# One step of a two-layer hybrid decoder on one core: v projected ahead of the row lists, the sample search, packing and list steps set further apart, and the sample queries copied right behind their rotation

## The chip, the cores and the metric

The kernel runs on one core of a Trainium2 chip. The metric is device time in microseconds (us) of one execution. TensorE is written PE, its weight loads PEld, VectorE DVE, ScalarE ACT, GpSimd POOL, and SyncE SP (which only issues transfers here).

## The reference, cut to what matters

A prompt of 256 tokens and 8 sequences with 4 new tokens each (288 columns in all) go through one attention layer, one convolution layer and two feed-forward blocks. The change lies in the attention layer, which chooses its keys:

```python
q, k, v, qi, ki, wi = project_attn(x, w_in)          # five projections of the same 288 tokens
q, k, qi, ki = rope_all(q, k, qi, ki, pos)           # partial rotation
ki_past = cache_ki[page_table].reshape(Bd, PAST_LEN, IDX_DIM)      # 2048 old index keys a sequence
...
dots = jnp.einsum('thd,sd->ths', qi, ki)             # index scores: 16 heads of 64
score = jnp.einsum('th,ths->ts', wi * IDX_W_SCALE, jax.nn.relu(dots))
_, idx = lax.top_k(jnp.where(causal, score, -jnp.inf), k_sel)      # 64 keys (prompt), 256 keys (samples)
...
k_s = jnp.where(in_past, cache_k[phys, off], k_new[new_idx])       # chosen rows of the paged cache
v_s = jnp.where(in_past, cache_v[phys, off], v_new[new_idx])
return attend_selected(q_s, k_s, v_s, valid)
```

For the 32 sample tokens the choice becomes a list of 256 cache rows each, and these rows (keys and values together, 1 MB a token) are gathered from memory.

## The kernel before, in words

**Matmuls.** Each weight matrix is split into a high and a low part, and three matmuls (L230, L231, L232) of 128x128 by 288 columns make one product. `pump` keeps weights ahead: SP loads a slab of 512 KB into `raw` (L147, five buffers), ACT makes the high part `wh` (L161), and DVE, or POOL where the slab's `pool` flag is set, makes the low part `wl` (L163; three buffers of each, made two slabs ahead). A slab of a 512-column group holds two k-tiles of four outputs, a slab of a v group four k-tiles of two: 24 matmuls either way. The v weights have 2 groups of 8 slabs, each q group has 8 slabs.

**Order by hand.** Every engine takes its instructions in program order. The program is one long sequence of groups: index key, k, two groups of index queries `qi`, four groups of q, and then v. Beside them run "lanes", lists of Python generators. After every small batch of matmuls `tick` gives each lane a credit, 0.3675 for a k-tile of one output (capped at 3.0 when it is saved up), and a generator goes on when its lane's credit is above zero; the number it yields is what its next step has to wait for. So a yield of 1.5 sets the next step four or five batches of three matmuls further on in the program. A q group hands out 64 batches, 23.52 credits. A v group would hand out three ticks for every four k-tiles of one output: 24 ticks, 8.82 credits. What is left in a lane at the end is emitted at once by `drain`, with no matmuls between its steps.

**The lanes at the change.** `rope_qi` rotates the index queries of one group on DVE, first the 32 sample columns, then the 256 prompt columns. `load_kx` asks SP for the 8 gathered parts of the index-key cache at fixed credits (`KXD`). `prompt_index` scores the prompt (two halves) and picks 64 keys in 16 rounds of `max` and `match_replace` (L1026, L1027), `TOPK` credits apart. `sample_index` copies the rotated sample queries into a block layout (L814, L817), makes 16 index dot products on PE (L839, each with an ACT relu and a weighted sum L830), then finds the 256th value of each row by 32 counting steps (DVE counts at L886, PE sums the counts over the partitions at L868, `BIS` credits apart), ranks ties, packs the chosen codes to the left in 9 steps (L943 to L946), shifts the four lists of a row together in 8 steps (L970, L971), turns them by PE (L977) into `idxS`, and calls `kv_load`, which has POOL issue two gathers (L657) for every token as far as buffers allow.

**After the drain** the stage's memory and PSUM banks are given back. `kv_load` goes on to 7 tiles, the two v groups run (L230 to L232 into `sc` and `m`, ACT copies to `vT`, PE transposes L1103, DVE copies L1105), then two more tiles reuse the memory of the low part of x (`kvx`, allowed only when v has been projected), and POOL clears `qz` and `PTz` (L1119). The prompt's attention is a generator too (`filler`): `HEAD` credits of it stand ahead of the sample loop, the rest inside it. The loop takes the 32 sample tokens in turn: four PE transposes twice a token (L1188), scores (L1209), and for every four tokens softmax and values (L1252). A tile's buffer is free when its values are done, and then the gather nine tokens further on is issued.

Of the kernel before, what the change touches and what calls it, by code (L numbers as in the profile page):

```python
# [7 lines left out]
F32 = mybir.dt.float32  # L8
# [4 lines left out]
AF = mybir.ActivationFunctionType  # L13
# [5 lines left out]
TP = 256  # L19
NS, TS = 8, 4  # L20
T = TP + NS * TS
# [16 lines left out]
NKVB = 3  # L38
# [3 lines left out]
SDEL = 6  # L42
TOPK = 1.0
DGP = 6.0
NDG = 10
CQ = 287
KXD = (54.0, 5.2)
PRW = (6.0, 14.0, 9.0)
DOT = 1.0
HEAD = 8.0  # L50
PEM, NACT = 3, 4
BIS = (1.3, 0.2)
ROPE = 0.5
# [482 lines left out]
def trunk(ctx, tc, a, o, stages=9):  # L536
    k = K(ctx, tc, a, o)
    nc = k.nc
# [7 lines left out]
    g_q = [k.add(Group([(win, QC + 512 * i, 512)], [128] * 4, NT, 2)) for i in range(4)]  # L546
    g_v = [k.add(Group([(win, VC + 256 * i, 256)], [128] * 2, NT, 4)) for i in range(2)]
    for g in g_q[1:3]:
        for s_ in g.slabs:
            s_.pool = True  # L550
# [56 lines left out]
    pb = pg  # L607
# [3 lines left out]
    bp = stB.enter_context(tc.tile_pool(name="idx", bufs=1))  # L611
# [29 lines left out]
    ident = k.ident = base.tile([128, 128], F32, name="ident")  # L641
# [40 lines left out]
    kxl, pl_ = Lane(), Lane()  # L682
# [3 lines left out]
    xin = lambda kk: (xh[:, kk, :T], xl[:, kk, :T])  # L686
# [5 lines left out]
    turned = []  # L692
# [10 lines left out]
    def rope_qi(gi):  # L703

        for c0, n in ((TP, T - TP), (0, TP)):
            wide = lambda v: cc(v)[:, None, c0:c0 + n].to_broadcast([128, 4, n])
            yield from rope(qi[:, 4 * gi:4 * gi + 4, c0:c0 + n], R[:, :, c0:c0 + n], wide("ci"), wide("si"), SHUF_I,
                            lambda: turned.append(gi))

# [27 lines left out]
    ps = k.gemm(g_idx[0], xin, pg)  # L737
# [8 lines left out]

    kvt = {"pos": 0, "done": 0, "cap": 4}
    RING = 4 + NKVB + 2
# [57 lines left out]

    def sample_index():
        while 1 not in turned:
            yield 0.3
        for s in range(2):  # L810
            for par in range(2):
                src = qi[par * 64:(par + 1) * 64, :, TP:].rearrange("p j (r s t) -> p r s j t", s=2, t=TS)[:, :, s]
                dst = qb[s * 64:(s + 1) * 64].rearrange("p r (s j e t) -> p r s j e t", s=2, e=2, t=TS)[:, :, s, :, par]
                nc.vector.tensor_copy(dst, src)  # L814
        kn = bp.tile([128, 4, TS], F32, name="kn")
        for s in range(2):
            nc.vector.tensor_copy(kn[s * 64:(s + 1) * 64],  # L817
                                  ki[s * 64:(s + 1) * 64, TP:].rearrange("p (r s t) -> p r s t", s=2, t=TS)[:, :, s])
        p = pb()
        nc.tensor.matmul(p[:, :32], cc("esel", 64, 80), kiw[64:80, TP:], start=True, stop=True)  # L820
# [62 lines left out]
        for bit in range(30, -1, -1):  # L883
# [32 lines left out]
        nc.vector.tensor_tensor_scan(rank, eq, eq, 0.0, OP.add, OP.max)  # L916
        yield 1.5

# [6 lines left out]
                                cc("blk", 96, 128).rearrange("p (b t) -> p b t", t=TS), op=OP.max)  # L925
        yield 1.5

# [12 lines left out]
        for b in range(9):  # L940
            s_ = 1 << b
            m = sp.tile([128, 512], I32, name="m_", tag="w", bufs=3)
            nc.vector.tensor_scalar(m, x_, 1 << (15 + b), None, op0=OP.bitwise_and)  # L943
            y = sp.tile([128, 512], I32, name="x_", tag="w", bufs=3)
            nc.vector.scalar_tensor_tensor(y, m, 0.0, x_, op0=OP.is_equal, op1=OP.mult)
            nc.vector.copy_predicated(y[:, :512 - s_], m[:, s_:], x_[:, s_:])  # L946
            x_ = y
            yield 2.4

# [17 lines left out]
        for b in range(8):  # L967
            s_ = 1 << b
            y = sp.tile([128, KSEL_S], F32, name="lst", tag="w", bufs=3)
            nc.vector.tensor_scalar(y, lst, b0[:, b:b + 1], None, op0=OP.mult)  # L970
            nc.vector.scalar_tensor_tensor(y[:, s_:], lst[:, :KSEL_S - s_], b1[:, b:b + 1], y[:, s_:],  # L971
                                           op0=OP.mult, op1=OP.add)
            lst = y
            yield 1.3
        p = pb()
# [91 lines left out]
    def post_q(h):  # L1067
        return lambda: nc.gpsimd.tensor_copy(qn[:, h], q[:, 4 * h:4 * h + 4, TP:].rearrange("p g t -> p t g"))

    for gi in range(4):  # L1070
        ps = k.gemm(g_q[gi], xin, pg)
        evac_rope(2 * gi + 2, ps, [q[:, 4 * gi + m] for m in range(4)], post_q(gi))
    k.drain(k.ev, k.bg2, k.bg, kxl, pl_)
    k.lanes.remove(kxl)
# [12 lines left out]
    def bank(n, bufs):  # L1087
        return pp.tile([128, 512], F32, name=n, bufs=bufs)

    kvt["B"], kvt["cap"] = kvB, 4 + NKVB  # L1090
    kv_load(0)
    for gi in range(2):
        n_ = ("sc", "m")[gi]
        ps = k.gemm(g_v[gi], xin, lambda: bank(n_, 2))
        vT = cp.tile([128, 2, T], F32, name="vT", tag="PT", bufs=2)
        for m in range(2):
            nc.scalar.activation(vT[:, m], ps[m][:, :T], AF.Copy)
        nc.sync.dma_start(o["v"].rearrange("(j p) t -> p j t", p=128)[:, 2 * gi:2 * gi + 2], vT)
        for tt in range(3):
            n = 128 if tt < 2 else 32  # L1100
            p = bank("tr", 3)
            for m in range(2):
                nc.tensor.transpose(p[:n, m * 128:m * 128 + 128], vT[:, m, tt * 128:tt * 128 + n], ident)  # L1103
            dst = vt[:, tt] if tt < 2 else vs
            nc.vector.tensor_copy(dst[:, 256 * gi:256 * gi + 256], p[:n, :256])  # L1105

# [759 lines left out]
```

## Time and profile before

| what | value |
|---|---|
| three timed runs | 2685.71, 2688.73, 2689.75 us; median 2688.73 |
| profiled execution | 2684.9 us; span from first to last instruction 2683.1 us |
| PE busy | 2568.1 us, 96% of the span |
| DVE, ACT, POOL busy | 1624.3, 1160.8, 615.2 us |
| mean granted TensorE clock | 0.984 of full speed |

The page cuts the span into 40 slices of 67 us. In PE's line of tenths the first seven slices read 8899688, all later ones but one 9; the granted clock falls below 9 tenths in the sixth slice alone. The attention layer is the first 470 us of the span, and all that the change touches is in it.

### The profile page before, as it was taken

To read this page: it belongs to the slowest core of one execution; us is meant where nothing else is said; L and a number is where in the kernel's file an instruction comes from. 1 tells how busy PE (TensorE), PEld (TensorE's weight loads), DVE (VectorE), ACT (ScalarE), POOL (GpSimd) and SP (SyncE) were. 2 spreads that over 40 slices of the span, in tenths; PEclk is the share of its full clock that TensorE was granted. 3 is DMA by queue.
4 is the path that set the end of the run, shared out by engine and by line. 5 is a ranking of instruction groups with operands and counts; after the bars stand their busy time and mean duration, and the time that the engine had idled before them with its cause. 6 is when DMAs were issued, how large, how long until landed. Compare 5 with 4: busy or idle time off the path is not lost.

```text
span 2683.1 us, 49547 instructions
## 1 busy us (share of the span) xinstructions
PE 2568.1 (96%) x19608; PEld 2464.8 (92%) x19608; DVE 1624.3 (61%) x2546; ACT 1160.8 (43%) x1801; POOL 615.2 (23%) x857
## 2 busy tenths in 40 slices
PE   8899688999999999999999999899999999999997
PEld 8779555999999999999998889899999999999997
DVE  4568443668666445555557888778655544555554
ACT  4333233456444334444446444656444333444434
POOL 1023324243222110111126444443111000111123
PEclk9999799999999999999999999999999999999999
DMA  9834636556554555555554766555555445555653
GB/s 342 181 87 131 227 131 244 185 168 197 162 172 156 167 166 165 159 172 164 158 165 128 201 161 175 171 157 161 171 165 165 165 160 164 172 165 159 167 169 106
DMA packets 410552, 454.90 MB, mean 170 GB/s; under 512 B 34816, under 2 KB 338608, under 8 KB 409168
## 3 DMA queue, kind: packets, MB, share of 16 engines
q1 hardware_dynamic: 397920, 400.66, 49.3%
q0 software_dynamic: 12400, 51.09, 5.7%
q8 instruction: 153, 2.51, 0.4%
q14 instruction: 79, 0.65, 0.1%
HBM read 438.37 MB, written 13.30 MB: 168 GB/s over the span
## 4 chain that ended last, share of the span: by engine, by line
PE 85%; DVE 4%; issue 3%; DMA 2%; POOL 2%; ACT 2%; SPq 1%; another core or an unknown queue 0%; ACTq 0%; DVEq 0%; POOLq 0%
PE pt L231 25%; PE pt L232 25%; PE pt L230 25%; PE pg L230 2%; PE pg L232 2%; PE pg L231 2%; DVE wl L163 1%; PE pt L1652 1%; ACT wh L161 1%; POOL kvt L657 1%; PE tr L1188 1%; DMA kvt<-kvc,idxS 1%; PE pg L839 1%; DMA xt<-spread 1%; PE m L1252 0%
## 5 line engine op out<-in xcount | busy, mean ns | idle before, releaser
L163 DVE TENSOR_TENSOR wl<-raw,wh 128x1024 fp32r<-128x1024 f32 (+2 forms) x709 | 883.9, 1250 | 816.5 <-ACT wh L161 796.2
L161 ACT ACTIVATE wh<-raw 128x1024 fp32r<-128x1024 f32 (+1 forms) x726 | 760.4, 1051 | 939.8 <-PE pt L231 684.0
L232 PE MATMUL pt<-xh,wl 128*128 128x288 f32 (+1 forms) x3520 | 1040.7, 296 | 5.4 <-DVE wl L163 5.4
L230 PE MATMUL pt<-xh,wh 128*128 128x288 f32 (+1 forms) x3520 | 1043.2, 296 | 0.8 <-ACT xh L1311 0.8
L231 PE MATMUL pt<-xl,wh 128*128 128x288 f32 (+1 forms) x3520 | 1043.1, 296 | 0.1
L232 PEld LDWEIGHTS pt<-xh,wl 128*128 128x128 f32 x3520 | 666.9, 189 | 6.6 <-DVE wl L163 6.6
L230 PEld LDWEIGHTS pt<-xh,wh 128*128 128x128 f32 x3520 | 664.0, 189 | 7.4 <-issue 5.4
L231 PEld LDWEIGHTS pt<-xl,wh 128*128 128x128 f32 x3520 | 664.7, 189 | 0.5 <-DVE xl L1312 0.3
L232 PE MATMUL pt<-hh,wl 128*128 128x288 f32 (+1 forms) x1664 | 495.3, 298 | 2.9 <-DVE wl L163 2.9
L231 PE MATMUL pt<-hl,wh 128*128 128x288 f32 (+1 forms) x1664 | 495.0, 297 | 0.0
L230 PE MATMUL pt<-hh,wh 128*128 128x288 f32 (+1 forms) x1664 | 493.2, 296 | 1.2 <-ACT wh L161 1.2
L232 PEld LDWEIGHTS pt<-hh,wl 128*128 128x128 f32 x1664 | 312.8, 188 | 3.9 <-DVE wl L163 3.9
L230 PEld LDWEIGHTS pt<-hh,wh 128*128 128x128 f32 x1664 | 313.8, 189 | 2.4 <-ACT wh L161 2.1
L231 PEld LDWEIGHTS pt<-hl,wh 128*128 128x128 f32 x1664 | 313.6, 188 | 0.2
L1427 POOL COPY sto<-gpad 128x2 f32<-128x2 f32 x88 | 82.0, 932 | 963.6 <-ACT gpad L1420 963.5
L230 PE MATMUL pg<-xh,wh 128*128 128x288 f32 (+1 forms) x464 | 148.4, 320 | 8.2 <-ACT wh L161 7.7
L232 PE MATMUL pg<-xh,wl 128*128 128x288 f32 (+1 forms) x464 | 139.6, 301 | 1.8 <-DVE wl L163 1.7
L231 PE MATMUL pg<-xl,wh 128*128 128x288 f32 (+1 forms) x464 | 139.8, 301 | 0.1
L1431 ACT ACTIVATE s<-y,pvec 128x304 f32<-128x304 f32 x88 | 48.4, 550 | 162.0 <-DVE y L1426 162.0
L230 PEld LDWEIGHTS pg<-xh,wh 128*128 128x128 f32 (+1 forms) x464 | 88.8, 191 | 18.0 <-issue 8.7
L305 POOL TENSOR_TENSOR lns<-lns,x 128x288 f32<-128x288 f32 x56 | 53.0, 947 | 184.4 <-DVE x L1340 176.9
L232 PEld LDWEIGHTS pg<-xh,wl 128*128 128x128 f32 (+1 forms) x464 | 89.0, 192 | 3.1 <-DVE wl L163 3.1
(389 smaller groups left out, 2428.2 us busy)
## 6 DMA issues: line engine op xcount, KB each, us to landing
raw<-w_ffn_gate SPq DMA_DIRECT2D x352, 256.0 KB, 2.9
raw<-w_ffn_up SPq DMA_DIRECT2D x352, 256.0 KB, 3.2
raw<-w_ffn_down SPq DMA_DIRECT2D x169, 512.0 KB, 3.9
raw<-w_attn_in SPq DMA_DIRECT2D x64, 512.0 KB, 5.4
raw<-w_pw SPq DMA_DIRECT2D x128, 256.0 KB, 4.4
raw<-w_attn_out SPq DMA_DIRECT2D x32, 512.0 KB, 4.3
raw<-w_pw SPq DMA_DIRECT2D x32, 512.0 KB, 4.2
xt<-spread SPq DMA_DIRECT2D x60, 136.0 KB, 3.1
```

What stands on the lines that cost most here:

```text
L161: nc.scalar.activation(wh[:, :n], r[:, :n], AF.Copy)
L163: eng.tensor_tensor(wl[:, :n], r[:, :n], wh[:, :n].bitcast(F32), op=OP.subtract)
L230: nc.tensor.matmul(out, wh[:, c:c + w], xh, start=st, stop=False)
L231: nc.tensor.matmul(out, wh[:, c:c + w], xl, start=False, stop=False)
L232: nc.tensor.matmul(out, wl[:, c:c + w], xh, start=False, stop=sp)
L305: nc.gpsimd.tensor_tensor(self.s1, self.s1, self.x[:, j], op=OP.add)
L657: nc.gpsimd.indirect_dma_start(out=out, out_offset=None, in_=src, in_offset=bass.IndirectOffsetOnAxis(ap=idx, axis=0))
L839: nc.tensor.matmul(p[:, :512], qb[:, pr], kx[pr][:, 512 * i:512 * i + 512], start=True, stop=True)
L1188: nc.tensor.transpose(p[:, h * 128:(h + 1) * 128], g[:, h * 128:(h + 1) * 128], ident)
L1427: nc.gpsimd.tensor_copy(sto[:, j, 0:2], gp[:, 256:258])
L1431: nc.scalar.activation(s[:, :304], y[:, :304], AF.Silu, bias=k.par(bc, j))
L1652: nc.tensor.matmul(p[32 * i:32 * i + 32, :TP], dg[:, i, m - PEM], xt[:, i, 4 * (m - PEM):4 * (m - PEM) + TP], start=m == PEM, stop=m == 7, ...
```

## The change

1. The v groups move from behind the drain to behind the four q groups, ahead of it. Their output goes to the memory of `qi`, and the transposes become a generator `turn_v` in a lane, with copies on ACT in place of DVE. The lists are drained after the second v group.
2. Distances in program order: search steps 1.3 + 0.2 to 1.6 + 0.3, ranking 1.5 to 2.5 and 1.5 to 2.0, packing 2.4 to 2.9, list steps 1.3 to 1.4, top-k rounds 1.0 to 1.6, and the index dot products 1.0 to 0.35, with a wait of 5.0 ahead of the first.
3. The sample queries' copies (L814, L817) are issued by `rope_qi` right after the sample columns of the second group, ahead of the prompt columns.
4. The eight loads of index keys are asked for from 53.0 on, 4.8 apart (before: 54.0 and 5.2).
5. The low parts of the first four slabs of the fourth q group are made on POOL. The copies `qn` of the sample queries (L1068) move from POOL to ACT.
6. `HEAD` goes from 8 to 10, and `kv_load` issues two tiles before the memory is given back, not four.

```diff
-TOPK = 1.0
+TOPK = 1.6
-KXD = (54.0, 5.2)
+KXD = (53.0, 4.8)
-DOT = 1.0
-HEAD = 8.0
+DOT = 0.35
+HEAD = 10.0
+DOTW = 5.0
-BIS = (1.3, 0.2)
+BIS = (1.6, 0.3)
...
-    for g in g_q[1:3]:
-        for s_ in g.slabs:
+    for g in g_q[1:]:
+        for s_ in g.slabs[:8 if g is not g_q[3] else 4]:
             s_.pool = True
...
-                            lambda: turned.append(gi))
+                            lambda: turned.append(gi) if c0 else None)
+            if c0 and gi:
+                sample_queries()
...
-    kvt = {"pos": 0, "done": 0, "cap": 4}
+    kvt = {"pos": 0, "done": 0, "cap": 2}
...
+    def sample_queries():
         for s in range(2):
             for par in range(2):
...
+    def sample_index():
+        while 1 not in turned:
+            yield 0.3
+        yield DOTW
...
         nc.vector.tensor_tensor_scan(rank, eq, eq, 0.0, OP.add, OP.max)
-        yield 1.5
+        yield 2.5
...
                                 cc("blk", 96, 128).rearrange("p (b t) -> p b t", t=TS), op=OP.max)
-        yield 1.5
+        yield 2.0
...
             x_ = y
-            yield 2.4
+            yield 2.9
...
             lst = y
-            yield 1.3
+            yield 1.4
...
-        return lambda: nc.gpsimd.tensor_copy(qn[:, h], q[:, 4 * h:4 * h + 4, TP:].rearrange("p g t -> p t g"))
+        return lambda: nc.scalar.activation(qn[:, h], q[:, 4 * h:4 * h + 4, TP:].rearrange("p g t -> p t g"), AF.Copy)
...
-    k.drain(k.ev, k.bg2, k.bg, kxl, pl_)
+    vT = bp.tile([128, 8, T], F32, name="qi")
+    def turn_v(gi):
+        for tt in range(3):
+            n = 128 if tt < 2 else 32
+            p = pb()
+            for m in range(2):
+                nc.tensor.transpose(p[:n, m * 128:m * 128 + 128], vT[:, 2 * gi + m, tt * 128:tt * 128 + n], ident)
+            dst = vt[:, tt] if tt < 2 else vs
+            nc.scalar.activation(dst[:, 256 * gi:256 * gi + 256], p[:n, :256], AF.Copy)
+            yield 0.6
+    for gi in range(2):
+        ps = k.gemm(g_v[gi], xin, pg)
+        for m in range(2):
+            nc.scalar.activation(vT[:, 2 * gi + m], ps[m][:, :T], AF.Copy)
+        nc.sync.dma_start(o["v"].rearrange("(j p) t -> p j t", p=128)[:, 2 * gi:2 * gi + 2], vT[:, 2 * gi:2 * gi + 2])
+        if gi:
+            k.drain(k.ev, k.bg2, kxl, pl_, k.bg)
+        pl_.append(turn_v(gi))
+    k.drain(pl_)
```

The v groups' old place, with their copies of `vT` on DVE, is taken out.

## Rows read from the trace of the kernel before

**Rows 1.** What PE waited for, first 400 us: us in total, times, longest

```profile
PE pg L977 <- DVE lst L970: 11.7, 1, 11.7
PE pg L839 <- issue: 8.9, 1, 8.9
...
PE pg L868 <- DVE scr L886: 5.3, 4, 3.5
PE pg L868 <- ACT x L726: 4.0, 1, 4.0
```

**Rows 2.** Stretches of 10 us: each engine's busy time, granted clock, DMA share, GB/s

```profile
110.00:120.00 10.00, 5.17 (x11) 3.13 (x12) 5.12 (x11) 1.19 (x2) 0.00 (x0) 0.54 0.28 69
...
220.00:230.00 10.00, 10.00 (x79) 10.00 (x78) 7.11 (x33) 3.18 (x3) 6.24 (x4) 1.00 0.50 139
...
240.00:250.00 10.00, 6.02 (x37) 5.81 (x37) 8.78 (x18) 5.11 (x11) 0.92 (x1) 0.87 0.31 97
...
260.00:270.00 10.00, 10.00 (x77) 10.00 (x77) 9.69 (x15) 3.73 (x5) 0.00 (x0) 1.00 0.48 134
...
300.00:310.00 10.00, 4.12 (x18) 3.53 (x18) 3.53 (x5) 2.60 (x4) 2.48 (x3) 0.60 0.94 343
```

**Rows 3.** DVE in order of time, 107 to 115 us: start, duration, instruction

```profile
107.75 0.29 DVE L695 STREAM_SHUFFLE rsh<-qi 128x128 f32<-128x128 f32 x1
...
112.53 1.22 DVE L699 TENSOR_TENSOR qi<-qi,rsh 128x1024 f32<-128x1024 f32 x1
113.68 0.92 DVE L814 COPY qiblk<-qi 64x128 f32<-64x128 f32 x4
```

**Rows 4.** DMA issues between 60 and 130 us, median to landing

```profile
kvt<-kid SPq DMA_DIRECT2D x8, 512.0 KB, 11.0
```

**Rows 5.** DVE by line and shape, 60 to 284 us: count, busy us, mean ns

```profile
L163 DVE TENSOR_TENSOR wl<-raw,wh 128x1024 fp32r<-128x1024 f32 x28 | 34.0, 1224 | 45.4 <-ACT wh L161 45.2
...
L1026 DVE MAX8 m<-pacc 128x8 f32<-128x256 f32 x8 | 3.4, 422 | 0.1
L1027 DVE MATCH_REPLACE8 pacc<-m,pacc 128x256 f32<-128x256 f32 x8 | 3.3, 410 | 0.0
```

**Rows 6.** DVE in order of time: a rotation, the list steps, the finished list

```profile
174.32 0.46 DVE L720 TENSOR_TENSOR rsh<-rsh,con 128x288 f32<-128x288 f32 x1
174.69 2.60 DVE L721 TENSOR_TENSOR rsh<-rsh,con 128x288 f32<-128x288 f32 x1
...
279.09 0.35 DVE L970 TENSOR_SCALAR lst<-lst,b 128x256 f32<-128x256 f32 x1
...
279.99 0.35 DVE L970 TENSOR_SCALAR lst<-lst,b 128x256 f32<-128x256 f32 x1
...
284.11 0.22 DVE L980 TENSOR_SCALAR idxS<-pg 128x64 int32<-128x64 f32 x1 [0.77 <-PE pg L977]
```

**Rows 7.** POOL in order of time: a low part, first and fourteenth gather, clearing

```profile
174.43 2.55 POOL L163 TENSOR_TENSOR wl<-raw,wh 128x1024 fp32r<-128x1024 f32 x1 [3.37 <-ACT wh L161]
...
284.62 1.79 POOL L657 DMA_INDIRECT kvt<-kvc,idxS  x1 [7.66 <-DVE idxS L980]
...
302.16 0.93 POOL L657 DMA_INDIRECT kvt<-kvc,idxS  x1 [0.31 <-issue]
...
327.58 0.58 POOL L1119 MEMSET qz<- 128x256 f32 x2
```

**Rows 8.** PE in order of time, from the first v matmul into the loop

```profile
284.48 0.58 PE L230 MATMUL sc<-xh,wh 128*128 128x288 f32 x1 [0.41 <-DVE idxS L980]
...
306.51 1.63 PE L1103 MATMUL tr<-ident,vT 128*128 128x128 f32 x6 [5.12 <-ACT vT L1097]
...
324.13 0.22 PE L1137 MATMUL tr<-pm,identN 128*128 128x128 bf16 x1
...
344.03 0.60 PE L1188 MATMUL tr<-ident,kvt 128*128 128x128 f32 x4
...
373.94 0.63 PE L1188 MATMUL tr<-ident,kvt 128*128 128x128 f32 x4 [0.47 <-DMA kvt<-kvc,idxS]
```

More of the change, by code (lines that the diff above doesn't have):

```diff
@@ L805, in prepare @@
         yield 0.1
-    def sample_index():
-        while 1 not in turned:
-            yield 0.3
+    kn = bp.tile([128, 4, TS], F32, name="kn")
+    def sample_queries():
         for s in range(2):
@@ L814, in sample_index @@
                 nc.vector.tensor_copy(dst, src)
-        kn = bp.tile([128, 4, TS], F32, name="kn")
         for s in range(2):
@@ L1088, in bank @@
         return pp.tile([128, 512], F32, name=n, bufs=bufs)
-    kvt["B"], kvt["cap"] = kvB, 4 + NKVB
+    kvt["B"] = kvB
+    kvt["cap"] = 4 + NKVB
     kv_load(0)
[L1092 to L1105, printed above, removed]
     ot = q
```

## The prediction

> **What bounds the kernel now.** I read the page first: PE is busy in nearly every slice except in the first 470 us, so I asked for stretches of 10 us there and then for what PE waited on. Four holes stand out. (1) PE does nothing for 8.9 us in front of the first index dot product, L839 [rows 1]; the releaser is not named, but DVE's order of time shows it: the rotation of the sample columns begins at 107.75, yet the copies that L839 needs come at 113.68 and end at 114.6, behind four long instructions on the prompt columns, of which the last stands in the rows [rows 3]. So the hole is from 105.9 to 114.8. The clock is granted at 0.54 in that stretch [rows 2]. (2) The counting search waits 5.3 us for its DVE counts [rows 1], at about 170 to 180 us, where search steps, top-k rounds and a rotation meet. (3) At 243 to 247 PE waits 4.0 us [rows 1]; the row names ACT, but the sum behind it needs the count of the packing scan, which DVE reaches late, as a rotation stands ahead of it; the clock is 0.87 there [rows 2]. (4) After the last q matmul PE waits 11.7 us for the list steps [rows 1]; the list is read out at 284.11 [rows 6], about 1 us behind the end of that wait, so q ends at about 271.3. Then come v and the gathers together: first v matmul at 284.48, first attention matmul at 324.13, 39.65 us for what is 192 matmuls and 12 transposes [rows 8]; in the stretch at 300 PE is busy 4.12 us of 10 while the DMA engines are at 0.94 [rows 2]: v's weights come in behind the gathers. The head of prompt attention takes from 324.13 to 344.03, and the tokens begin [rows 8].
>
> **The change part by part.** I count credits from the first q matmul: q ends at 4 x 23.52 = 94.1, v would end at 94.1 + 2 x 8.82 = 111.7. Where matmuls run free PE does 77 in 10 us [rows 2], so a slab of 24 takes 3.12 us, a credit of a q group 1.06 us and one of a v group 1.41 us.
>
> *Copies behind the sample rotation, dots later.* The lane has 3.0 saved, so the 5.0 leaves 2.0 credits, then 1.5: the first dot stands 3.7 credits or 3.9 us of matmuls behind 105.5, at 109.4. The sample rotation is four instructions of about 0.29 us from 107.75 on, it ends at about 108.9, and the copies take 0.92 more [rows 3]: ready at about 109.9. Of 8.9 us some 0.5 is left: 8.4 gained. The prompt's rotation moves back by the copies' 1.3 us; the next low part behind it is due only after two slabs and a dozen dots. The clock: a mean of 0.54 over 10 us, between levels of 1.0 and 0.5, is 9.2 us at the low level (1.2 GHz), so PE worked from 114.8 to 120 at half speed and lost 2.6 us; with no hole before it I give that back. Sum 11.0. Bounds: 8.4, if the clock falls all the same, and 12.
>
> *Index-key loads.* Load 8 moves from credit 14.0 to 10.2. What is moved past is SP's queue: a key load lands 11.0 us after issue [rows 4], and a raw slab of the same size behind it waits. Matmuls of slabs already landed hide it: 0, at worst one load of 512 KB ahead of one slab, at the 343 GB/s of the stretch at 300 [rows 2] 1.5 us.
>
> *Search and top-k.* With low parts on POOL the search alone keeps DVE busy 7.11 us of 10 [rows 2], at 1.5 credits a step; at 1.9 that is 5.6. A late top-k round is 422 + 410 ns [rows 5], 0.78 of DVE's time at 1.0 credit, 0.49 at 1.6. Together 1.49 becomes 1.05: still over one, and over a longer overlap. The search starts at credit 12.8 (dots end at 11.6, as load 8 is at 10.2), before at 19.2; top-k runs to 36.5, before 26.9. The excess before, 7.7 credits at about 1.2 us by 0.49, is 4.5 us plus q's rotation with its 2.60 us instruction. After: 12 credits by 0.05, under 1 us, two low parts of 1.22 us each [rows 5] near the start, and the same rotation, some 5 us, against slack of about 1.9 us in a step: 3 us left of 5.3. I take a gain of 2; bounds -5 (all of the surplus of a longer overlap on PE) and +5.3.
>
> *Four slabs to POOL.* Each takes 1.22 us from DVE [rows 5] and 2.4 to 2.6 us of POOL [rows 7], which has 3.1 a slab. The row says something else too: while POOL had its low part from 174.43 on, DVE's L721 took 2.60 us, where its like just before took 0.46 [rows 6, 7]: 2.15 us lost. The Trainium skill, "SBUF — State Buffer", section "Who interferes with whom", has it that a DVE instruction with two SBUF inputs and a GpSimd one that reads SBUF block each other, the later one fully; the trace agrees in this pair. By that rule four more slabs could cost four such blocks, 8.6 us of DVE, where the saving is 4.9; by the rows it happened to one of the rotation's instructions with 16 such slabs around, so I keep the gain above and count this in its lower bound.
>
> *Ranking later.* The packing scan comes at credit 79.7 (12.8 + 60.8 + 1.6 + 2.5 + 2.0), 9 behind the start of q's last group, out of the rotation's way, where before it fell at 71.5, one credit behind it. The 4.0 us go, and about 0.5 of clock: 4.5. Bounds 0 and 5.3.
>
> *Packing, lists, and v.* First packing step at 81.2, then 9 x 2.9 and 1.2: lists begin at 108.5, and at 111.7 three of eight are out. Five are left at 0.90 us [rows 6], with one under way 5.4 in place of 11.7: 6.3 gained. Before, packing and low parts filled DVE to 9.69 of 10 [rows 2]; 2.9 instead of 2.4 makes room for the low parts that remain, and in v a slab gives only 2.2 credits in 3.12 us. Bounds 0 (nothing shortened) and 9.
> v itself: 192 / 7.7 = 24.9 us, transposes at 1.63 for six at the low clock [rows 8], together 2.5: 27.4 for 39.65, 12.2 gained, rounded to 12. The weights no longer meet the gathers, since these are issued after. Bounds 6 (if the 5.9 us hole of the stretch at 300 comes back) and 13. The copies of v and q on ACT (3.18 us of 10 busy at 220 [rows 2]) cost nothing; if ACT were late, low parts would be late next.
>
> *Bare gathers.* Now nothing but the head covers them. The list should be ready at about 286 (284.1 - 11 - 2 - 4.5 - 6.3 + 24.9 + 0.8), 2 us later than before, and the head starts 2 us behind that, not 40. POOL needs 17.54 / 13 = 1.35 us a gather [rows 7], 18 of them and the clearing of `qz`: done at 286 + 24.9 + 0.6 = 311.5. The head takes 19.9 us [rows 8], plus the two further yields of `HEAD` = 10: about 24, ending at 312. So the tokens begin at about 311, the two conditions level. The two yields stood inside the first token before: 0, bounds -4 and 0. The first nine tokens took 344.03 to 373.94 [rows 8]; nine tiles and 3.7 MB of the next weights at 343 GB/s [rows 2] are 13.1 MB in 38 us, so tile 8 lands by about 327 and is wanted at 336: 0. From tile 9 on a gather waits for its buffer in both kernels.
>
> Sum: 11 + 2 + 4.5 + 6.3 + 12 = 35.8. From the profiled 2684.9 that is 2649.1; the median of the runs is 3.8 higher, 2652.9 by the same gain. I take 2651.
>
> **The rivals.**
> *DVE stays the bound*: search and top-k overlap longer, POOL blocks DVE more often, and holes 2 and 3 are as deep as before or deeper. For: 1.05 is over one [rows 2, 5]. Against: in q's second and third group DVE had a third of its time free. With -5 and 0 for those terms the sum is 24.3: 2662. Chance 0.17.
> *The list's tail stays*: DVE comes to the end of v late, 11.7 us again: 2657. For: 9.69 of 10 busy. Chance 0.10.
> *The first hole stays*, moved: the dots wait for the key loads or for the weights behind them. For: 11.0 us to landing [rows 4]. Sum 24.8: 2662. Chance 0.06.
> *Tiles late*: with 200 GB/s in place of 343, 13.1 MB take 65 us, tile 8 lands at 351 and not 336, 15 us: 2666. Against: the rate of the same gathers [rows 2]. Chance 0.08.
> *Slower*: the gathers are held up one by one by DVE, as L721 was by POOL, now that the head's softmax runs beside all 18. At 2.15 us more each [rows 6] `qz` is cleared at 286 + 18 x 3.5 + 0.6 = 350, six behind the 344 of before, and the tokens' own gathers suffer too: about 2695. It decides from 32.5 / 18 = 1.8 us more a gather. The Trainium skill, on the same page under "SBUF: two separate sides", warns of this: descriptors of GpSimd's transfers cannot be written while DVE holds the shared ports. Against it: the gathers came at an even 1.35 us [rows 7] with DVE at work on low parts, though not on softmax. Chance 0.04.
> *Nothing comes of it*, as tokens wait for tiles by all that was won: 0.02.
>
> **How the numbers follow.** My forecast has 0.53: 2651, its own range 2643 to 2658. The rivals at 2657 to 2666 are taken in, and a little on the lower side for bounds not reached (12, 5.3, 5.3, 9 and 13 give 44.6, 2640): 2640 to 2667 leaves out under 2 in 10. About 0.2%, 5 us, is what a measurement of this kernel can tell. Faster 0.93, the same 0.03, slower 0.04.
>
> **What the changed profile would show.** No wait of L839 over 1 us near 106 and a granted clock of 1.0 to 130; waits of L868 summing to 3 or 4 us; the wait of L977 at 5 to 6 us, around 280; v's matmuls in 25 us with no stretch under 9 of 10; gathers from about 286 in an even row; first L1188 near 311, and everything behind the attention loop some 36 us earlier. The prediction is wrong if DVE reads 9 of 10 and more from 115 to 150 with PE below, if L977 waits 10 us, if POOL's gathers spread beyond 1.5 us, or if L1188 waits for DMA in its first nine tokens.

## The result, and the profile after

The changed kernel takes 2661.59 us (median; 2660.16 to 2664.78), the kernel before, beside it, 2688.94 us: ratio 0.9902, 95% interval 0.9885 to 0.9919, or 27.3 us. I had said 2651, a gain of 35.8. The profiled execution takes 2662.52 us (before 2684.9), its span is 2660.7, its mean clock 0.986.

After the change the lines are numbered up to 16 higher: low parts L164, index dots L846, counts L893 with their sums L875, list steps L977, list matmul L984, `idxS` L987, gathers L658; in the head the scores are L1154, row maxima L1155, transposes L1180, values L1176; key transposes are L1204. What PE waits for, first 400 us, against [rows 1]:

```profile
PE q L1176 <- ACT PT L1182: 17.7, 4, 12.3
...
PE pg L984 <- DVE lst L977: 5.1, 1, 5.1
PE pg L875 <- DVE scr L893: 3.9, 5, 0.9
...
PE pg L875 <- DVE cnt L938: 1.5, 1, 1.5
```

The wait of the index dots (8.9 us) is gone, the list wait is 5.1 where it was 11.7, and the counting sums wait 3.9 + 1.5 and another 0.8 in a shorter row, 6.2 in all for 10.3 (5.3 + 4.0 and another 1.0). Above all of them stands a wait that the kernel before did not have in this size: 12.3 us in the head of the prompt's attention. Stretches of 10 us, against [rows 2]:

```profile
110.00:120.00 10.00, 9.99 (x43) 5.53 (x44) 6.41 (x9) 4.31 (x7) 0.00 (x0) 1.00 0.76 164
...
240.00:250.00 10.00, 10.00 (x78) 10.00 (x77) 9.77 (x14) 3.47 (x4) 0.00 (x0) 1.00 0.46 130
260.00:270.00 10.00, 10.00 (x76) 9.72 (x76) 9.04 (x14) 5.50 (x9) 0.00 (x0) 1.00 0.37 102
300.00:310.00 10.00, 1.16 (x6) 0.76 (x5) 0.00 (x0) 0.00 (x0) 7.13 (x10) 0.67 1.03 420
```

The clock is whole where it had been 0.54 and 0.87. The first gap closes with the copies of the sample queries, which DVE now makes at 108.87 and not at 113.68 [rows 3]:

```profile
108.87 0.93 DVE L817 COPY qiblk<-qi 64x128 f32<-64x128 f32 x4
```

From 300 to 310 PE is busy 1.16 us, and DVE and ACT not at all, while the DMA engines move 420 GB/s. PE in order of time (start, duration, instruction; in brackets the idle time before it and its releaser), against [rows 8]:

```profile
283.32 1.06 PE L984 MATMUL pg<-con,lst 128*128 128x32 f32 x4 [5.14 <-DVE lst L977]
...
286.18 0.27 PE L1153 MATMUL tr<-pm,identN 128*128 128x128 bf16 x1 [0.46 <-ACT vt L1091]
...
299.56 0.74 PE L1154 MATMUL tr<-kT,x 128*128 128x128 f32 x2
300.10 1.06 PE L1180 MATMUL tr<-ident,P 128*128 128x128 f32 x4
313.47 2.08 PE L1176 MATMUL q<-PT,vt 128*128 128x512 f32 x2 [12.31 <-ACT PT L1182]
...
324.86 0.67 PE L1204 MATMUL tr<-ident,kvt 128*128 128x128 f32 x4
```

The list is turned at 283.32, the head begins 2.9 us later, and the first key transpose comes 38.7 us after that, where I had 24. DVE in the hole, in order of time:

```profile
295.38 0.95 DVE L1165 TENSOR_SCALAR P<-P,sm 128x128 f32<-128x128 f32 x4
310.41 0.69 DVE L1155 TENSOR_REDUCE mx<-tr 128x4 f32<-128x512 f32 x1 [14.08 <-remote]
```

L1155 reads what the L1154 matmuls wrote, and these had ended at 300.3. It starts 10 us later, and its row names no engine of the core as releaser ("remote": the profile knows none). The trace also records when an engine's reports arrive, the semaphore updates by which it tells the others that an instruction is done. PE's five reports of the matmuls L1154 and L1180, which end from 300.31 to 301.16, are recorded from 310.39 to 310.52, all at once. So DVE did not wait for work that was late, but for word of work that was done.

POOL and the tiles were as forecast; its order of time, against [rows 7]:

```profile
284.93 1.06 POOL L658 DMA_INDIRECT kvt<-kvc,idxS  x1 [53.89 <-DVE idxS L987]
...
306.27 0.94 POOL L658 DMA_INDIRECT kvx<-kvc,idxS  x1 [0.31 <-issue]
307.20 0.58 POOL L1135 MEMSET qz<- 128x256 f32 x2
```

18 gathers in 21.3 us, 1.25 from one to the next.

### The profile page after: what moved, and what is told of

Read it like the earlier page. It is cut to its first block, busy times and chain, and to the rows that moved or that the text cites. A ratio compares the mean times of both kernels' runs of the same rounds, so it can differ in the third digit from the quotient of the medians.

```text
span 2660.7 us, 49550 instructions
## 1 busy us (share of the span) xinstructions
PE 2561.8 (96%) x19608; PEld 2459.0 (92%) x19608; DVE 1617.9 (61%) x2536; ACT 1164.6 (44%) x1811; POOL 623.8 (23%) x857
## 4 chain that ended last, share of the span: by engine, by line
PE 87%; DVE 5%; DMA 2%; POOL 2%; ACT 2%; issue 1%; another core or an unknown queue 1%; SPq 0%; DVEq 0%; ACTq 0%; POOLq 0%
PE pt L233 25%; PE pt L232 25%; PE pt L231 25%; PE pg L231 2%; PE pg L233 2%; PE pg L232 2%; DVE wl L164 1%; PE tr L1204 1%; PE pt L1668 1%; ACT wh L162 1%; PE m L1268 1%; PE sc L1225 1%; DMA xt<-spread 1%; PE pg L846 1%
## 5 line engine op out<-in xcount | busy, mean ns | idle before, releaser
L164 DVE TENSOR_TENSOR wl<-raw,wh 128x1024 fp32r<-128x1024 f32 (+2 forms) x705 | 880.3, 1252 | 778.9 <-ACT wh L162 763.7
L231 PE MATMUL pg<-xh,wh 128*128 128x288 f32 (+1 forms) x528 | 166.4, 315 | 8.1 <-ACT wh L162 8.1
L233 PE MATMUL pg<-xh,wl 128*128 128x288 f32 (+1 forms) x528 | 157.6, 298 | 1.5 <-DVE wl L164 1.4
L232 PE MATMUL pg<-xl,wh 128*128 128x288 f32 (+1 forms) x528 | 157.4, 298 | 0.0
L231 PEld LDWEIGHTS pg<-xh,wh 128*128 128x128 f32 (+1 forms) x528 | 99.8, 189 | 17.3 <-issue 8.4
L233 PEld LDWEIGHTS pg<-xh,wl 128*128 128x128 f32 (+1 forms) x528 | 99.9, 189 | 2.8 <-DVE wl L164 2.8
L232 PEld LDWEIGHTS pg<-xl,wh 128*128 128x128 f32 (+1 forms) x528 | 99.9, 189 | 2.4 <-issue 2.4
```

What stands on the lines that cost most here:

```text
L164: eng.tensor_tensor(wl[:, :n], r[:, :n], wh[:, :n].bitcast(F32), op=OP.subtract)
L231: nc.tensor.matmul(out, wh[:, c:c + w], xh, start=st, stop=False)
L232: nc.tensor.matmul(out, wh[:, c:c + w], xl, start=False, stop=False)
L233: nc.tensor.matmul(out, wl[:, c:c + w], xh, start=False, stop=sp)
```

## The experiments

The result above is group 1, the first pair of runs. Twelve kernels then ran in three more groups, each on one chip beside runs of the kernel before. That kernel took 2688.94 us in the first group, 2669.3 in the second, 2684.35 in the third and 2670.94 in the fourth, so times are compared inside a group, and across groups by ratios alone. The changed kernel itself was not run in the second group, and the kernel before was traced in the first and third alone. Where the groups differ is one of the findings. A table of places, read from PE's order of time in each trace (us from the start of the span; "next layer" is the first matmul of the output projection):

| kernel | group | first index dot | list turned | head begins | first key transpose | next layer |
|---|---|---|---|---|---|---|
| before | 1 | 114.83 | 283.01 | 324.13 | 344.03 | 468.37 |
| changed | 1 | 110.01 | 283.32 | 286.18 | 324.86 | 448.03 |
| changed, HEAD 8 | 2 | 110.92 | 284.14 | 286.99 | 308.54 | 428.24 |
| changed, gathers paced | 2 | 110.70 | 283.98 | 286.84 | 314.75 | 430.53 |
| before, early copies alone | 2 | 109.72 | 270.06 | 303.63 | 324.77 | 439.17 |
| changed, v at its old place | 2 | 110.54 | 271.78 | 304.86 | 332.67 | 450.43 |
| before | 3 | 115.60 | 284.66 | 324.25 | 343.16 | 468.67 |
| changed | 3 | 110.67 | 285.40 | 288.26 | 324.86 | 447.11 |
| changed, HEAD 8 | 3 | 110.28 | 283.53 | 286.38 | 318.86 | 449.67 |
| changed, late copies | 3 | 114.61 | 291.47 | 294.33 | 332.11 | 455.23 |
| changed | 4 | 110.77 | 284.02 | 286.88 | 315.01 | 429.56 |
| changed, gathers paced | 4 | 111.09 | 284.36 | 287.21 | 315.17 | 431.38 |
| changed, paced, HEAD 8 | 4 | 110.97 | 285.69 | 288.55 | 311.52 | 427.68 |
| changed, old distances | 4 | 110.29 | 276.65 | 299.89 | 327.83 | 442.67 |

**Group 2: the head, and two halves of the change.** The head with its old share:

```diff
-HEAD = 10.0
+HEAD = 8.0
```

> The changed kernel with HEAD back at 8.0. Theory A, the two further yields of the head cost what the trace shows ahead of the first token and are hardly given back inside the loop: the first key transposes come 5 to 6 us earlier, the loop is 1 us longer, total 4 to 5 us less than the changed kernel, about 2657. Rival, as the prediction had it, the two yields only change place: the loop is longer by as much as the head is shorter, total unchanged within 1 us. The hole of 12 us in the head stays in both.

Measured: 2640.31 us, ratio 0.9895 (0.9878 to 0.9911). The head takes 21.6 us, and the wait of 12 us, which I had expected to stay, is not there: the longest in front of the values is 2.6.

The gathers spread out, two tiles ahead of the head and two more after each softmax (the copy of `sm` makes POOL wait for it):

```diff
-    kvt["cap"] = 4 + NKVB
-    kv_load(0)
...
-    kvt["B2"], kvt["cap"] = base.tile([128, 2, 2, 1024], F32, name="kvx", tag="xl"), RING
-    kv_load(0)
+    kvt["B2"] = base.tile([128, 2, 2, 1024], F32, name="kvx", tag="xl")
+    pace = cp.tile([128, 4], F32, name="pace", bufs=1)
...
+            if kvt["cap"] < RING:
+                nc.gpsimd.tensor_copy(pace, sm)
+                kvt["cap"] = min(RING, kvt["cap"] + 2)
+                kv_load(0)
```

> The changed kernel with the first nine tiles' gathers paced: two tiles at once, then two more after each of the first four softmax units of the head (POOL copies a result of DVE first, so it really waits), and qz and PTz cleared ahead of them. Theory A, the 12 us hole in the head comes from 18 gathers standing in the DMA queues at once, and updates of TensorE reach DVE late while they drain: the wait of L1176 for L1182 falls from 17.7 us to under 8, the head from 38.7 to about 28, total about 2651. Rival B, the hole is a wait of its own at the third unit of the head (memory or a bank given over): it stays at 12 us, total unchanged, 2661. Rival C, paced gathers come too late: the hole goes, but L1204 waits for DMA in the first nine tokens by as much.

Measured: 2643.95 us, ratio 0.9906 (0.9889 to 0.9923), head 27.9. By itself this says nothing on the cause: HEAD 8 had lost the hole in this group too, with all 18 gathers in one burst.

The kernel before, with early copies, closer dots and earlier key loads alone:

```diff
-KXD = (54.0, 5.2)
+KXD = (53.0, 4.8)
-DOT = 1.0
+DOT = 0.35
+DOTW = 5.0
...
+            if c0 and gi:
+                sample_queries()
```

> The kernel before with only the early copies, the dots' distances and the key loads of the change. Theory: the hole of 8.9 us at 106 goes and the clock stays up, 11 us; the search begins some 6 credits earlier and so the list's tail is shorter by about 5 us as well: 2672 to 2675. Rival, the first hole is only moved (the dots wait for key loads, or the low parts behind the rotation are late): under 5 us gained, 2684 or more.

Measured: 2658.74 us, ratio 0.9962 (0.9950 to 0.9975): 10.6 us, where my term was 11.0. PE's waits in that kernel:

```profile
PE pg L984 <- DVE lst L977: 9.8, 1, 9.8
...
PE pg L875 <- DVE scr L893: 4.1, 5, 1.3
```

The list comes 12.9 us earlier than in the kernel before of group 1 (no trace of that kernel in this group): 11.0, and 1.9 because the list wait shrinks from 11.7 to 9.8.

The changed kernel with v back behind the drain:

```diff
-    vT = bp.tile([128, 8, T], F32, name="qi")
-    def turn_v(gi):
...
-    for gi in range(2):
-        ps = k.gemm(g_v[gi], xin, pg)
...
+    k.drain(k.ev, k.bg2, k.bg, kxl, pl_)
...
+    for gi in range(2):
+        n_ = ("sc", "m")[gi]
+        ps = k.gemm(g_v[gi], xin, lambda: bank(n_, 2))
```

> The changed kernel with v projected behind the drain again, beside the gathers, all else kept. Theory: with the wider spacing five packing steps and eight list steps are left at the end of q, a tail of about 17 us instead of 5; v takes 40 us beside the gathers instead of 28, but the 12 us hole in the head is then inside v's stretch: net 12 to 16 us slower than the changed kernel, 2674 to 2678. Rival, moving v is worth only the tail's cover and the hole appears in the head as well: 24 us slower, 2686.

Measured: 2661.44 us, ratio 0.9972 (0.9962 to 0.9981), which cannot be told from the early copies alone: what is set further apart has to be paid in the tail. By ratios it is 18 us above the changed kernel, where I expected 12 to 16 (the tail about 17 us, as it came, and 40 us for v, where it took less). Its list wait, and three of its stretches behind it:

```profile
PE pg L984 <- DVE lst L977: 18.0, 1, 18.0
```

```profile
280.00:290.00 10.00, 9.61 (x74) 9.32 (x73) 4.21 (x6) 3.89 (x5) 7.87 (x8) 1.00 0.98 379
290.00:300.00 10.00, 10.00 (x77) 10.00 (x76) 2.91 (x4) 2.12 (x2) 2.67 (x3) 1.00 0.99 360
300.00:310.00 10.00, 6.10 (x47) 5.23 (x45) 5.85 (x7) 2.26 (x6) 6.00 (x8) 1.00 0.88 299
```

Here v's matmuls run beside the gathers at 360 to 379 GB/s, as in [rows 2], and PE has no hole. From the list's matmul to the head it takes 33.1 us (33.6 with the early copies alone), in the kernel before 41.1. So v's weights behind the gathers were not what held PE in the kernel before.

**Group 3: the hole again.** The kernel before once more, unchanged:

> The kernel before, unchanged, for a trace on the chip that the other runs of this call use. Theory A (while a burst of gathers drains, other engines' reports come late, and whether they do depends on the chip): if this chip is like that of the second group of runs, no row of 290 to 310 us names an unknown releaser with 10 us, first v matmul to first attention matmul takes 32 to 33 us in place of 39.65, and the execution takes about 2669 us; if it is like the chip of the first pair, the row is there again and it takes about 2686. Theory B (the stretch at 300 us belongs to the program: v's weights behind the gathers): 39 to 40 us on either chip.

Measured: 2682.82 us in the one run; 39.6 us from list to head. ACT in order of time, first the kernel before from which the prediction was made, then this run:

```profile
293.76 1.06 ACT L161 ACTIVATE wh<-raw 128x1024 fp32r<-128x1024 f32 x1 [3.18 <-PE sc L232]
305.11 1.06 ACT L161 ACTIVATE wh<-raw 128x1024 fp32r<-128x1024 f32 x1 [10.29 <-remote]
```

```profile
306.05 1.06 ACT L161 ACTIVATE wh<-raw 128x1024 fp32r<-128x1024 f32 x1 [9.59 <-remote]
```

Ten microseconds without a named releaser in the middle of v: the same kind of row as in the head of the changed kernel. In the first of the two traces, PE's matmuls ahead of it had ended at 295.88 and 296.01, and their reports are recorded at 305.08 and 305.12. The weights had long been there. v has eight slabs (two groups of four; 192 matmuls), and the DMA issues of the kernel before from 250 to 272 us, ahead of the first gather at 284.62, hold seven of them, with 3.7 us to landing:

```profile
raw<-w_attn_in SPq DMA_DIRECT2D x7, 512.0 KB, 3.7
```

The slab of the late row had landed by 272.22.

The changed kernel once more:

> The changed kernel, unchanged. Theory A on a chip without late reports: the hole of 12.3 us in front of the value matmuls shrinks to about 7, as in the runs with HEAD 8 and with paced gathers; head 28 us in place of 38.7 (HEAD 8 took 21.6, two more yields some 6); time about 2646, ratio to before 0.991. On a chip with late reports as in the first pair: head 38 to 39 us, ratio 0.990. Theory B (the hole is an own wait of the head's third unit, of the program's order): 12 us again on either chip, ratio about 0.995 beside a before of 2669.

Measured: 2659.28 us, ratio 0.9904 (0.9887 to 0.9921). The wait in front of the values is 10.9 us, and DVE's L1155 again starts behind 12.69 us put down to "remote".

HEAD 8 once more (the same edit, beside the changed kernel of this group):

> The changed kernel with HEAD 8 in place of 10, beside the changed kernel on the same chip. Theory that the two further yields stand on the path, since the tiles wait in their buffers by then: 5 to 6 us quicker than the changed kernel, some 1 given back in the loop: 4 to 5 us. Rival (what my prediction said: the yields stood inside the first tokens before, and cost nothing): within 1 us.

Measured: 2660.47 us, ratio 0.9903 (0.9885 to 0.9921): no difference, where I expected 4 to 5 us. The head has the hole too (L1155 behind 13.99 us put down to "remote") and takes 32.5 us for 36.6. The first key transpose comes 6 us earlier than with HEAD 10, 1.9 of it from the stretch ahead of the head, but the next layer 2.6 us later. Its stretches in the tokens, and a row of ACT there:

```profile
360.00:370.00 10.00, 6.76 (x83) 3.99 (x81) 3.26 (x11) 2.21 (x7) 6.39 (x7) 1.00 0.91 307
370.00:380.00 10.00, 9.06 (x75) 5.88 (x76) 3.09 (x9) 3.10 (x6) 0.95 (x2) 0.66 0.30 114
```

```profile
370.29 0.60 ACT L1209 ACTIVATE KT<-tr 128x512 f32<-128x512 f32 x1 [1.55 <-remote]
```

A row of that kind stands in the next burst of gathers; PE loses 3.2 us from 360 to 370, and then the clock falls to 0.66.

The sample queries' copies back behind the rotation of the prompt columns:

```diff
-            if c0 and gi:
-                sample_queries()
...
         yield DOTW
+        sample_queries()
```

> The changed kernel with the sample queries' copies issued behind the rotation of the prompt columns again (and behind the wait of 0.3 steps), everything else as changed. Theory that the copies' place made the first hole: a wait of PE of 3.5 us or more in front of the first index dot product (copies ready at about 114, dots placed at 109.5), clock low behind it, first dot near 114.5, time 7 to 11 us above the changed kernel. Rival (the wider distances and the lane's saved credit alone closed it, or a later wait takes up the delay, as v's end and the list are slack): below 3 us.

Measured: 2669.48 us, ratio 0.9943 (0.9926 to 0.9959), 10.2 us above the changed kernel. PE's wait, and DVE in order of time:

```profile
PE pg L845 <- issue: 4.7, 1, 4.7
```

```profile
108.57 1.34 DVE L696 STREAM_SHUFFLE rsh<-qi 128x1024 f32<-128x1024 f32 x1
...
113.48 0.92 DVE L815 COPY qiblk<-qi 64x128 f32<-64x128 f32 x4
```

The first dot comes at 114.61, 3.9 us late, and the clock of the stretch from 110 to 120 reads 0.66. So the copies' place made the first hole; distances do not close it.

**Group 4: without the hole.** The changed kernel a third time:

> The changed kernel, unchanged, beside the three that follow on one chip. If the chip has late reports: ratio 0.990, a wait of 10 to 12 us in front of the value matmuls of the head. If it has none: ratio about 0.991 and 7 us there.

Measured: 2644.15 us, ratio 0.9904 (0.9886 to 0.9922), head 28.1. DVE's same instruction, and the stretch at 300:

```profile
301.05 0.69 DVE L1155 TENSOR_REDUCE mx<-tr 128x4 f32<-128x512 f32 x1 [4.02 <-PE tr L1154]
```

```profile
300.00:310.00 10.00, 7.27 (x27) 5.08 (x26) 2.77 (x9) 2.80 (x11) 7.65 (x11) 0.53 1.03 418
```

The same program, the same burst (418 GB/s for 420), and L1155 now starts as soon as its matmuls end. The rival, an own wait of the program, falls with this row.

The two paced kernels:

> The changed kernel with its gathers spread over the head: two tiles first, two more after each softmax, and the clearing of the zero tiles ahead of them. Theory A (reports come late while a burst of 18 gathers drains): on a chip with late reports the wait in front of the value matmuls falls from 11 or 12 us to about 7, the head from 38 us to 28 to 30, and the time is 6 to 10 us below the changed kernel; on a chip without them the two are within 2 us. Rival (the lateness has nothing to do with the burst, or pacing only moves it into the first tokens): the same as the changed kernel on a chip with late reports, or above it.

> The same with HEAD 8. Where the two yields stand on the path (as on the chip where HEAD 8 alone took 21.6 us of head), 4 to 6 us below the paced one; where the loop gives it back (on the other chip the head was 6 us shorter and the loop 8.5 us longer), the same within 2 us. Rival: above the paced one, as the tiles behind the second are not there when the tokens begin earlier, 2 us or more of waits for gathers.

```diff
-HEAD = 10.0
+HEAD = 8.0
```

Measured: 2644.54 us, ratio 0.9905 (0.9888 to 0.9923), and with HEAD 8 2642.18 us, ratio 0.9897 (0.9879 to 0.9914). Neither can be told from the changed kernel. In this pair HEAD 8 shortens the head by 5.0 us (28.0 to 23.0) and leaves the loop of the tokens at 116.2 us; the 2.4 us between the two times are within the noise. As no reports came late in this group, whether pacing cures that stays open.

The changed kernel with all distances as before:

```diff
-TOPK = 1.6
+TOPK = 1.0
-BIS = (1.6, 0.3)
+BIS = (1.3, 0.2)
...
-        yield 2.5
+        yield 1.5
...
-        yield 2.0
+        yield 1.5
...
-            yield 2.9
+            yield 2.4
...
-            yield 1.4
+            yield 1.3
```

> The changed kernel with all distances of search, ranking, packing, list steps and top-k as before (1.0; 1.3 and 0.2; 1.5; 2.4; 1.3), so with v ahead of the lists, early copies and POOL slabs alone. My prediction's terms for spacing: search 2 us, ranking 4.5 us; the tail is covered either way, and shorter steps leave it nothing, so up to 5 us come back: waits of the count matmuls 9 to 11 us in sum (changed: 6.2), the list wait 0 to 2 us (changed: 5.1), time 0 to 4 us above the changed kernel. Rival (closer steps need only be paid where DVE is full, and v covers the lists): 3 to 6 us below it. Rival (spacing carries the gain): 8 us or more above.

Measured: 2655.33 us, ratio 0.9946 (0.9929 to 0.9964), 11.2 us above the changed kernel: neither my terms (up to 5) nor the rival below it, but the one that lets the distances carry the gain. PE's waits from 150 to 300 us, then four stretches, of this kernel and of the changed one in the same group:

```profile
PE pg L875 <- DVE scr L893: 4.1, 5, 1.3
PE pg L984 <- DVE lst L977: 3.5, 1, 3.5
PE pg L875 <- DVE cnt L938: 3.4, 1, 3.4
PE pg L875 <- ACT wh L162: 2.4, 1, 2.4
...
PE pg L875 <- DVE yes L897: 1.3, 1, 1.3
```

```profile
160.00:170.00 10.00, 7.03 (x49) 6.10 (x47) 9.58 (x36) 4.61 (x11) 4.97 (x2) 1.00 0.20 56
170.00:180.00 10.00, 7.76 (x37) 7.79 (x38) 7.21 (x32) 3.39 (x6) 2.36 (x1) 0.66 0.35 104
220.00:230.00 10.00, 6.91 (x52) 6.59 (x50) 9.22 (x15) 2.12 (x2) 5.46 (x3) 1.00 0.42 118
230.00:240.00 10.00, 9.51 (x51) 9.51 (x52) 9.01 (x15) 4.18 (x10) 2.37 (x1) 0.66 0.29 94
```

```profile
160.00:170.00 10.00, 8.31 (x63) 7.90 (x62) 9.24 (x37) 6.46 (x14) 6.33 (x3) 1.00 0.48 147
170.00:180.00 10.00, 9.59 (x73) 9.36 (x73) 9.48 (x42) 3.18 (x3) 4.94 (x4) 1.00 0.38 109
220.00:230.00 10.00, 10.00 (x79) 10.00 (x79) 7.26 (x29) 7.93 (x16) 5.60 (x4) 1.00 0.36 106
230.00:240.00 10.00, 8.49 (x64) 8.25 (x64) 9.48 (x16) 2.53 (x3) 1.75 (x1) 1.00 0.72 211
```

The counting sums wait 11.2 us, a little over the 9 to 11 expected, for 6.2; the list wait is 3.5, where I expected 0 to 2. What I had not priced is the clock. In this trace both stretches with 3 us of idle time are followed by one at 0.66: between levels of 1.0 and 0.5 that is 6.8 us at 1.2 GHz, or up to 3.4 us of work lost, twice. v's first matmul comes at 263.68 for 252.27, and 5.0 + 2 x 3.4 is 11.8 for these 11.4 us. (The list is turned earlier than in the changed kernel, but in the midst of v, so the head still waits for v.) The changed kernel is idle for up to 1.7 us in these stretches, and its clock holds.

Such a loss does not always follow. The early copies alone have the same waits up to 172 us (the longest 2.4 us) and keep their clock:

```profile
160.00:170.00 10.00, 6.49 (x44) 5.54 (x43) 9.59 (x35) 4.71 (x11) 4.46 (x2) 1.00 0.25 64
170.00:180.00 10.00, 8.24 (x61) 7.88 (x61) 8.46 (x40) 2.98 (x5) 5.13 (x3) 1.00 0.30 96
```

And the changed kernel waits 1.5 us at 238 in every group that has it; the stretch behind reads 1.00 in groups 1 and 4, but in group 3

```profile
240.00:250.00 10.00, 10.00 (x69) 10.00 (x68) 8.63 (x12) 2.80 (x3) 0.00 (x0) 0.88 0.38 105
```

So the 5.0 us of waits belong to the distances. How much of the clock's part belongs to them is not shown.

## Why the prediction was right in sum, and which step was wrong

**Copies, dots, key loads.** Right: 11.0 forecast, 10.6 with that part alone, 10.2 with the copies put back.

**Search, ranking, POOL slabs.** Right in mechanism: DVE's collisions shrink, and the sums' waits fall by 4.1. Mis-sized: 6.5 us for search and ranking, against 11.2 for all distances. With the four slabs on POOL and the old distances the sums wait 11.2, so it is the distances that shrink the waits. My term priced waits and 0.5 of clock; in that trace two stretches at half speed come on top, which the same waits did not bring in the kernel with the early copies alone. The block by POOL happened once again, as one row of the changed kernel shows for DVE, and one for POOL:

```profile
195.36 2.51 DVE L726 TENSOR_TENSOR rsh<-rsh 128x288 f32<-128x288 f32 x1
```

```profile
195.18 2.38 POOL L164 TENSOR_TENSOR wl<-raw,wh 128x1024 fp32r<-128x1024 f32 x1 [2.73 <-ACT wh L162]
```

L726 takes 0.46 us elsewhere, and here it ends 0.3 us behind POOL's low part. By the rule of the Trainium skill cited in the prediction ("SBUF — State Buffer", "Who interferes with whom") this is the shared port; the trace agrees, and the four more slabs did not multiply it: no other rotation instruction was blocked.

**List tail.** Right: 5.4 forecast, 5.1 measured. But it hangs together with the distances. v at its old place with the new distances brings nothing over the early copies alone (18.0 us of tail; ratio 0.9972 for 0.9962); v ahead with the old distances brings some 4 us (0.9946), which is no more than the noise of the two ratios; both bring 15 (0.9904).

**v: 12 us, as "the weights no longer meet the gathers".** This is the step that failed. The length of v held within some 2 us: its 192 matmuls take 26.6 us in the changed kernel of group 4, with six of the transposes among them, and the head begins 2.9 us behind the list's matmul, 29.5 together, where I had 27.4 for matmuls and transposes.

```profile
252.27 0.29 PE L231 MATMUL pg<-xh,wh 128*128 128x288 f32 x1
...
278.59 0.30 PE L233 MATMUL pg<-xh,wl 128*128 128x288 f32 x1
```

But the 5.9 us hole that I took out of [rows 2, 8] is not of v's weights: seven of their eight slabs had landed before the first gather, and in group 2, v at its old place runs beside the same gathers without the hole. It is ACT's row with 10.29 us put down to nobody, behind reports of PE that came 9 us late, and it goes with the burst of gathers, wherever that stands.

Where the hole occurs (groups 1 and 3), v wins 11.6 and 10.1 of its 12 (41.1 and 39.6 to 29.5), but the hole comes back in the head: 38.7 us and, from 288.26 to 324.86, 36.6 us, where the same program has 28.1 in group 4. Where it does not occur (groups 2 and 4), v wins 3.6, from 33.1 between list and head to 29.5. Of these, 2.1 are clock: behind the list wait of 18.0 us, v's first 4.2 us run at 1.2 GHz, as its matmuls start 0.24 us apart until 277.46 and 0.13 after. Either way some 8 to 11 of the 36 us were not to be had, and so the ratio is the same, 0.9902, 0.9904 and 0.9904. That v's 12 nearly came out in group 1 is luck: what was taken from v stood in the head.

**Bare gathers and head: 24 us, two yields at 0.** The gathers were quick and even, so the rival by which DVE holds them up fell: 1.25 us each with the softmax beside them. The head alone takes 28.1 without the hole, where I had 24. I had 4.1 for the two yields; they are 28.1 - 21.6 = 6.5 us between groups 4 and 2, 5.0 in the paced pair and 4.1 in group 3. In time they cost nothing that can be measured: the tokens' loop is 5.1 us shorter with HEAD 10 in groups 2 and 4 (114.6 for 119.7), 8.6 in group 3 (122.2 for 130.8), and no shorter in the paced pair. The bounds I had set for it (-4 and 0) hold it.

**The sum**, where no hole disturbs: 10.6 for the copies; of 24.8 for the rest, v falls 8.4 short and the yields cost 6.5 - 5.1 = 1.4, which leaves 15.0. Together 25.6, where 26.8 was measured (20.8 to 30.4 by the interval of the ratio). The term for the distances was too small, but they are paid only together with v's place, and the interaction hides that in this sum. The range held because it took in the rivals at 2657 to 2666, not because the terms were right one by one. Three of the prediction's own figures are off, without weight in the sum: from credit 12.8 to 36.5 search and top-k overlap for 23.7 credits, not 12 (1.3 us of surplus, not under 1); the 24.9 for the gathers has the 0.6 for the clearing in it already; and the 2640 for all upper bounds is counted from the profiled 2684.9, from the median it is 2644.

## What to carry to other kernels

Before a hole is put down to a transfer, look at the row of the instruction that starts late: its inputs may long be there, and then moving the transfer only moves the hole. Distances in a hand-written order and cover for its tail are one edit: here one alone was worth some 4 us, within the noise, the other alone nothing that could be measured, both 15. A hole can be paid twice, as the clock may be low behind it (two of 3 us in a trace of the old distances, each before a stretch at 0.66); but the same waits left the clock whole in another trace, so only the wait itself can be counted on beforehand.

## What the runs showed of the hardware

While a burst of gathers of 0.5 MB drains, at 343 to 420 GB/s, an engine may see the end of another engine's finished instruction some 10 us late: L1155 started at 310.41 on matmuls that ended at 300.3 and were reported at 310.39, L161 at 305.11 on one that ended at 295.9 and was reported at 305.08. Each of the six traces of groups 1 and 3 has one such wait of 9 us or more, in its first burst of gathers. But the burst alone is not enough: the eight traces of groups 2 and 4 have none, in the changed kernel of group 4 at 418 GB/s. The kernel before took 2684 to 2689 us where it occurred and 2669 to 2671 where it did not; each group was of one kind throughout. The third and fourth groups carry the same chip number, so that it belongs to a chip is not shown. What decides it, and whether spacing the gathers out would cure it, stays open.

The clock does not follow from the length of a hole alone: in one and the same program, 1.5 us of waiting at 238 us are followed by a stretch at 1.00 in groups 1 and 4 and by one at 0.88 in group 3.

The Trainium skill ("SBUF — State Buffer", "SBUF: two separate sides") has it that transfers and compute cannot slow each other at the memory's ports. The rows do not speak against that: the instruction that was late ran no longer than elsewhere (L1155 0.69 us in both traces); it started later.
